# A windowed attention kernel: first q in two transfers, the other loads held behind it, the spare v copied last, and GpSimd drained behind its last store

## The chip, the cores and the metric

The kernel runs on one core of one Trainium2 chip. The metric is the device time of one execution in microseconds (us). Times are quoted as medians with the number of runs. The kernel before took 962.15 us (median of 3 runs, 961.51 to 962.47).

Engine names are those of the profile: PE (matrix multiply), DVE (VectorE), ACT (ScalarE), POOL (GpSimd), SP (SyncE). "Landing" means the moment when the last of the 16 semaphore increments of a transfer arrives; the trace records each increment with its time. A "hole" is idle time of the 16 DMA engines, given as their mean idle share summed over time; the "tail" is the time from the last landing to the end of the span, and the "span" is the length of the profiled run.

## The reference, cut to what matters

```python
B, S, D, W = 4, 4096, 1536, 64          # q, k, v: (B, S, D) float32
q_w, k_w, v_w = (x.reshape(B, S // W, W, D) for x in (q, k, v))
logits = einsum('bnwd,bnud->bnwu', q_w, k_w) * D ** -0.5
attn = softmax(logits)                  # over each window of 64
out = einsum('bnwu,bnud->bnwd', attn, v_w)   # float32
```

Every window of 64 rows attends only to itself. There are 16384 rows; each row of q, k and v is read once and each row of the output written once, so the work per byte is small.

## The kernel before

The rows are cut into N = 32 units of 512 rows. For each unit PE transposes q and k (12 groups `g`, 6 of q and then 6 of k), forms the logits, ACT takes the exponential, PE multiplies by v, and DVE and ACT scale the result into one of three output buffers. DVE copies the even groups out of PSUM (the buffers `tp` into which PE writes), ACT the odd ones. GpSimd issues the loads, which cast from float32 to float16 on the way, and the stores. Loads of q, k and v for the next unit go into the buffers as they become free.

Three units (1, 2 and 31) get their v through another buffer, "spare v", because at that moment `v16` is still in use. DVE copies it into `v16`. Where this copy stands in DVE's order is one subject of the change:

```python
def vector_unit(u):
    ve = nc.vector
    for g in range(0, 2 * DC, 2):                 # DC = 6: g = 0, 2, ..., 10
        copy_out(ve, ve.tensor_copy, u, g)
        if g == DC - 2:                           # after the last q group of DVE
            src = {1: staged(1, 0), 2: vs, N - 1: vs}.get(u)
            if src is not None:
                ve.wait_ge(*((d_v1, 16) if u == 1 else (d_vs, 16 if u == 2 else 32)))
                ve.wait_ge(p_o[0], 6 * u)
                ve.wait_ge(p_o[1], 6 * u)
                ve.tensor_copy(out=v16[:, :, :], in_=src[:, :, :]).then_inc(g_v, 1)
    # ... reciprocals and scaling of the output (cut)
```

The start. The first q comes as raw float32 through SyncE into an output buffer and is cast by DVE and ACT; all other first loads are issued by GpSimd at once:

```python
with tc.tile_critical():
    nc.sync.dma_start(
        out=slots(outs[0], 0, SLOTS, SLOTS), in_=rows(qf, 0, SLOTS, SLOTS)
    ).then_inc(d_raw, 16)
    load("k", 0, k16, d_k)
    load("v", 0, v16, d_v)
    # ... ident (cut)
    load("q", 1, staged(2, 0), d_q1)
    load("k", 1, staged(2, 1), d_k1)
    load("v", 1, staged(1, 0), d_v1)
    load("v", 2, vs, d_vs)
    # ...
    for a, eng in enumerate((nc.vector, nc.scalar)):
        eng.wait_ge(d_raw, 16)
        copy = nc.scalar.copy if a else nc.vector.tensor_copy
        for i in range(a, SLOTS, 2):
            copy(out=q16[:, i, :], in_=outs[0][:, i, :]).then_inc(c_q[a], 1)
```

The end. The last unit's result goes out in five pieces (two by GpSimd, three by SyncE), SyncE waits for every store, the critical block closes (this drains the engines), and a second block clears the semaphores:

```python
    # still inside the first block; gp = nc.gpsimd, sy = nc.sync
    gp.dma_start(out=rows(of, base, R, R), in_=slots(o, 0, R, R)).then_inc(d_l[0], 16)
    # ... waits (cut)
    gp.dma_start(out=half[:, 0, :], in_=o[:, R, :]).then_inc(d_l[1], 16)
    # ... three stores of 256 KB by sy, waits of sy for all stores (cut)
with tc.tile_critical():
    # ...
    nc.gpsimd.sem_clear(range(lo, hi + 1))
```

The softmax here doesn't subtract the row's maximum and nothing guards it: scores larger than these inputs give would overflow.

## Time and profile before

| What | Value | Where it is read |
|---|---|---|
| time | 962.15 us | median of 3 runs |
| span of the profiled run | 960.4 us | head of the page |
| DMA busy | 9 tenths in 39 of 40 slices | slice strip |
| PE, ACT, DVE busy | 65%, 36%, 31% | busy table |
| HBM traffic | 302 MB read, 101 MB written, 419 GB/s | queue table |

First, the DMA strip of the page (busy tenths of each 1/40 of the span) and the line of the software queue in the queue table (packets, MB, share of the time of 16 engines), and the line of the chain that ended last, by engine:

```profile
DMA  9999999999999999999999999999999999999993
...
q0 software_dynamic: 26496, 249.31, 99.0%
...
DMA 3%; PE 3%; DVE 1%; ACT 1%; issue 0%; POOL 0%; ACTq 0%
```

The DMA strip shows 9 in every slice but the last. With the same bytes moved at the same rate, such a kernel can be shortened only where the DMA is not busy. So one looks at the edges. Here is the end, as stretches of time: start and end, length, busy time of PE, PEld, DVE, ACT and POOL with the number of instructions, granted clock of PE, DMA share, GB/s.

```profile
932.00:934.00 2.00, 2.00 (x20) 1.84 (x19) 0.69 (x1) 0.06 (x1) 0.00 (x0) 1.00 0.95 406
934.00:936.00 2.00, 2.00 (x20) 1.69 (x19) 0.00 (x0) 0.61 (x1) 0.00 (x0) 1.00 0.35 147
...
942.00:944.00 2.00, 1.45 (x8) 0.19 (x2) 1.22 (x3) 0.39 (x1) 0.00 (x0) 1.00 0.00 0
...
952.00:954.00 2.00, 0.00 (x0) 0.00 (x0) 0.00 (x0) 0.00 (x0) 0.00 (x0) 0.50 0.71 263
954.00:960.00 6.00, 0.00 (x0) 0.00 (x0) 0.00 (x0) 0.00 (x0) 0.00 (x0) 0.50 0.00 0
```

Two stretches stand out: from 934 to 945 the DMA has almost nothing to do while PE is still computing the last unit, and from 954 to the end no engine has any work. The reason for the first stands in the order of time of the last unit (start, length, engine, line, operation, operands, and in brackets the idle time before it and what ended it):

```profile
919.73 0.61 ACT L206 COPY xk<-tp 128x512 f32<-128x512 f32 x1 [1.26 <-PE tp L139]
...
925.54 1.76 DVE L232 COPY v<-vs 128x6144 f16<-128x6144 f16 x1 [7.42 <-DMA vs<-in_v_dram]
927.22 0.68 DVE L206 COPY xk<-tp 128x512 f32<-128x512 f32 x1
...
928.05 1.08 PE L139 MATMUL tp<-ident,k 128*128 128x128 f32 x4 [8.36 <-DVE xk L206]
...
944.58 0.57 POOL L372 DMA_DIRECT2D out_dram<-out  x1 [29.05 <-PE o L114]
```

DVE waits 7.42 us for v with k's copies behind it, and PE waits 8.36 us for the k copy, although nothing in k needs v.

The reason for the second stretch is a wait of SyncE, in the view of waits (engine and line, who was waited for, us in total, times, longest):

```profile
SPq L293 <- POOLq L293: 4.1, 1, 4.1
```

This is SyncE waiting for GpSimd's drain at the close of the block. The trace has the drain as a record of 4.31 us, from 954.25 to 958.56, directly behind the last landing (953.96).

The start, and GpSimd's issues of the third unit's q and of the fourth's (same columns):

```profile
0.96 0.38 SPq L295 DMA_DIRECT2D out<-in_q_dram  x1
...
1.48 0.67 POOL L107 DMA_DIRECT2D k<-in_k_dram  x1 [1.03 <-SPq L293]
...
16.59 1.28 ACT L322 ACT_TABLE_LOAD   x1 [16.59 <-DMA out<-in_q_dram]
...
20.80 5.83 PE L139 MATMUL tp<-ident,q 128*128 128x128 f32 x24 [20.80 <-SPq L334]
...
52.63 1.36 POOL L107 DMA_DIRECT2D q<-in_q_dram  x1 [46.93 <-PE tp L139]
...
76.46 1.78 POOL L107 DMA_DIRECT2D q<-in_q_dram  x1 [15.59 <-PE tp L139]
```

Raw q lands only at 16.5 us because it shares the engines with k's load, and the two q issues take 1.4 and 1.8 us instead of the usual 0.54. DVE copies the spare v at these moments (52.12 to 53.87 and 76.38 to 78.13 in the trace). The Trainium skill describes this ("SBUF — State Buffer", section "SBUF: two separate sides", the "DVE blocks DMA" trap): GpSimd cannot write descriptors while certain DVE copies hold the port that both share. The trace agrees: the two issues end 0.12 and 0.11 us after the copies do. Near 54 and 79 us the DMA has holes of together about 1.2 us (idle share summed over 0.05 us bins: 0.68 in 50 to 58, 0.48 in 74 to 82).

### The profile page before, as it was taken

How to read it: one execution, taken by the hardware profiler on the slowest of the kernel's cores; microseconds unless marked ns; L12 is line 12 of the kernel's file. 1: busy time of each engine (PE TensorE's matmuls, PEld its weight loads, DVE VectorE, ACT ScalarE, POOL GpSimd, SP SyncE). 2: the span in 40 equal slices, each digit the busy share in tenths (PEclk: the TensorE clock that was granted, in tenths of full speed). 3: DMA queues.
4: the chain of work that ended last, by engine and by line, in shares of the span. 5: the costliest groups of instructions: out<-in, count | busy, mean ns of one | idle time of the engine just before them, and what ended most of it. 6: DMA issues, size and time to landing. Idle time of an engine off the chain costs nothing. (4 is left out here: it accounts for less than half of the span.)

```text
span 960.4 us, 10207 instructions
## 1 busy us (share of the span) xinstructions
PE 627.1 (65%) x4096; PEld 348.2 (36%) x3328; DVE 300.8 (31%) x524; ACT 341.0 (36%) x643; POOL 82.8 (9%) x133
## 2 busy tenths in 40 slices
PE   1777767666667666676666676666776666866652
PEld 1444444323444233443233442334432334422340
DVE  1444323332233322233222333222333223332232
ACT  1444334333333333343333333333433333333312
POOL 1011111010111000110100110001100001100100
PEclk9999899898899898998888998989988989888978
DMA  9999999999999999999999999999999999999993
GB/s 256 215 203 254 278 283 278 281 250 249 281 282 277 275 236 268 280 281 280 259 242 279 281 279 277 246 257 281 281 280 272 241 268 282 282 276 256 243 327 139
DMA packets 27090, 253.40 MB, mean 264 GB/s; under 512 B 2112, under 2 KB 2112, under 8 KB 10816
## 3 DMA queue, kind: packets, MB, share of 16 engines
q0 software_dynamic: 26496, 249.31, 99.0%
q1 hardware_dynamic: 576, 3.93, 1.1%
q14 instruction: 16, 0.13, 0.0%
q8 instruction: 2, 0.03, 0.0%
HBM read 301.99 MB, written 100.66 MB: 419 GB/s over the span
## 5 line engine op out<-in xcount | busy, mean ns | idle before, releaser
L114 PE MATMUL o<-v,et 128*128 128x512 f16 x768 | 255.0, 451 | 208.9 <-PEq L178 153.8
L279 ACT ACTIVATE out<-o,rs 128x512 f32<-128x512 f32 x192 | 127.1, 686 | 273.3 <-DVE rs L240 195.2
L155 PE MATMUL lt<-xq,xk 128*128 128x256 f16 x1536 | 195.8, 275 | 0.0
L181 PEld LDWEIGHTS <-et 128*128 128x128 f16 x256 | 28.9, 113 | 414.7 <-issue 409.1
L155 PEld LDWEIGHTS lt<-xq,xk 128*128 128x128 f16 x1536 | 148.9, 97 | 23.4
L240 DVE RECIPROCAL rs<-sp 128x1 f32<-128x1 f32 x128 | 21.6, 169 | 430.3 <-PE sp L114 430.3
L139 PE MATMUL tp<-ident,q 128*128 128x128 f32 x768 | 104.7, 281 | 70.3 <-DVE xq L206 49.5
L249 DVE TENSOR_SCALAR out<-o,rs 128x512 f32<-128x512 f32 x192 | 138.4, 748 | 16.8 <-PE o L114 10.5
L139 PE MATMUL tp<-ident,k 128*128 128x128 f32 x768 | 113.1, 277 | 40.1 <-DVE xk L206 22.6
L139 PEld LDWEIGHTS tp<-ident,q 128*128 128x128 f32 x768 | 87.2, 144 | 103.5 <-issue 80.2
L206 ACT COPY xk<-tp 128x512 f32<-128x512 f32 x96 | 58.9, 614 | 166.4 <-PE tp L139 166.4
L265 ACT ACTIVATE et<-lt,zeros 32x128 f16<-32x128 f32 x256 | 91.7, 358 | 56.2 <-PE lt L155 53.0
L139 PEld LDWEIGHTS tp<-ident,k 128*128 128x128 f32 x768 | 87.1, 141 | 55.7 <-issue 53.9
L206 DVE COPY xk<-tp 128x512 f32<-128x512 f32 x96 | 66.4, 692 | 118.6 <-PE tp L139 118.6
L206 ACT COPY xq<-tp 128x512 f32<-128x512 f32 x96 | 59.1, 616 | 93.5 <-PE tp L139 93.5
L206 DVE COPY xq<-tp 128x512 f32<-128x512 f32 x96 | 66.1, 689 | 56.9 <-PE tp L139 56.9
L107 POOL DMA_DIRECT2D v<-in_v_dram x29 | 20.8, 716 | 461.4 <-PE o L114 461.4
L114 PE MATMUL sp<-ones,et 128*128 128x1 f16 x256 | 46.1, 180 | 0.0
L107 POOL DMA_DIRECT2D q<-in_q_dram x30 | 18.3, 610 | 170.3 <-PE tp L139 170.3
L107 POOL DMA_DIRECT2D k<-in_k_dram x31 | 16.9, 545 | 183.9 <-PE tp L139 182.9
L289 POOL DMA_DIRECT2D out_dram<-out x31 | 22.1, 713 | 17.9 <-DVE out L249 16.8
L322 ACT ACT_TABLE_LOAD x1 | 1.3, 1283 | 16.6 <-DMA out<-in_q_dram 16.6
(21 smaller groups left out, 19.5 us busy)
## 6 DMA issues: line engine op xcount, KB each, us to landing
out_dram<-out POOLq DMA_DIRECT2D x31, 3072.0 KB, 29.2
k<-in_k_dram POOLq DMA_DIRECT2D x31, 1536.0 KB, 22.3
q<-in_q_dram POOLq DMA_DIRECT2D x30, 1536.0 KB, 21.5
v<-in_v_dram POOLq DMA_DIRECT2D x29, 1536.0 KB, 18.9
out<-in_q_dram SPq DMA_DIRECT2D x1, 3072.0 KB, 15.6
vs<-in_v_dram POOLq DMA_DIRECT2D x2, 1536.0 KB, 39.6
out<-in_q_dram POOLq DMA_DIRECT2D x1, 1536.0 KB, 30.1
out<-in_k_dram POOLq DMA_DIRECT2D x1, 1536.0 KB, 36.8
```

The costliest lines, as they stand in the source:

```text
L107: nc.gpsimd.dma_start(out=slots(dst, 0, SLOTS, r), in_=rows(src, u * UR, SLOTS, r)).then_inc(s, 16)
L114: return nc.tensor.add_instruction(mybir.InstMatmult(name=nc.get_next_instruction_name(), engine=PE, ins=[low(rhs), low(w)], outs=[low(o)] ...
L139: ins = nc.tensor.transpose(tps[g % 2][:, r, j, :], pairs[:, c * P : (c + 1) * P], ident[:, :])
L155: ins = nc.tensor.matmul(lts[h][:, r, :, :], lhsT=halves(xk, c)[:, r, h, :, w], rhs=halves(xq, c)[:, :, h, :, w], start=(c == 0 and w == 0 ...
L181: ld = nc.tensor.ldweights(w)
L206: copy(out=dst, in_=tps[g % 2][:, :, :, :]).then_inc(f_c[g % 4], 1)
L240: ve.reciprocal(out=rs[:, n : n + 1], in_=sp[:, n : n + 1]).then_inc(n_r, 1)
L249: ve.tensor_scalar_mul(scaled(u, n, j), ops[j][:, :], scalar1=rs[:, n : n + 1]),
L265: ins = sc.activation(ets[h][s, :, :, s], lts[h][s, :, :, s], EXP, bias=zeros[s, :], scale=scale)
L279: sc.activation(scaled(u, n, j), ops[j][:, :], COPY, bias=0.0, scale=rs[:, n : n + 1]),
L289: gp.dma_start(out=rows(of, u * UR, SLOTS, R), in_=slots(outs[u % NO], 0, SLOTS, R)).then_inc(d_o[u % NO], 16)
L322: copy(out=q16[:, i, :], in_=outs[0][:, i, :]).then_inc(c_q[a], 1)
```

## The change

The intent: get q in first and start PE early; keep DVE's k copies from waiting behind v; let GpSimd's drain run while the last stores fly, and drop one barrier.

```diff
+    # start: q in halves, all other loads behind the first half, table load early
-        nc.sync.dma_start(
-            out=slots(outs[0], 0, SLOTS, SLOTS), in_=rows(qf, 0, SLOTS, SLOTS)
-        ).then_inc(d_raw, 16)
+        raw = rows(qf, 0, SLOTS, SLOTS).rearrange("p h (r d) -> p (h r) d", d=D)
+        for i, s in enumerate((d_r0, d_r1)):
+            sl = slice(2 * i, 2 * i + 2)
+            nc.sync.dma_start(out=outs[0][:, sl, :], in_=raw[:, sl, :]).then_inc(s, 16)
+        nc.gpsimd.wait_ge(d_r0, 16)
         load("k", 0, k16, d_k)
@@
+        nc.scalar.activation(rs[:, 0:1], zeros[:, :], EXP, bias=zeros[:, :], scale=1.0)
         for a, eng in enumerate((nc.vector, nc.scalar)):
-            eng.wait_ge(d_raw, 16)
             for i in range(a, SLOTS, 2):
+                eng.wait_ge(d_r1 if i > 1 else d_r0, 16)
@@ vector_unit: spare v behind all of DVE's copies
         for g in range(0, 2 * DC, 2):
             copy_out(ve, ve.tensor_copy, u, g)
-            if g == DC - 2:
-                src = {1: staged(1, 0), 2: vs, N - 1: vs}.get(u)
-                # ... waits and copy
+        src = {1: staged(1, 0), 2: vs, N - 1: vs}.get(u)
+        # ... the same waits and copy
@@ end: one block, drain behind GpSimd's last store
-    with tc.tile_critical():
+    with tc.tile_critical(no_gpsimd_drain=True):
@@
         gp.dma_start(out=half[:, 0, :], in_=o[:, R, :]).then_inc(d_l[1], 16)
+        gp.drain()
@@
             sy.wait_ge(d_l[i], 16)
-
-    with tc.tile_critical():
+        sy.sem_inc(done, 1)
+        gp.wait_ge(done, 1)
```

(The comment line at the top of the diff is an explanation, and semaphore names are cut.)

## The prediction

> **What bounds the kernel.** The DMA. The slice strip gives it 9 tenths in 39 of 40 slices, the queue table 99.0% for the software queue; PE is busy 65%. The bytes (302 MB read, 101 written) don't change, so only the edges can move.
>
> **The edges now**, from windows of 1 and 2 us: (a) no DMA until 2 us, then full; (b) holes of about 0.6 us at 54 and 0.4 us at 78 to 80; (c) most engines run dry at 934, share near 0 from 940 to 945; (d) last landing 954.0, then 6.4 us to the span's end (960.4).
>
> **Start.** Raw q shares the engines with the first k load and lands at 16.5 us; first transpose 20.8. Alone and split, its halves should land near 7 and 11 us, with the table load (1.28 us) out of the way: first transpose near 13. But k lands no earlier (same bytes ahead of it) and unit 1's q, k, v follow in the queue, so unit 0 ends only about 3 us sooner. That is enough to issue the next q before the queue empties, without a VectorE copy beside it (the issues at 52.6 and 76.5 took 1.36 and 1.78 us, usually 0.54), so holes (b) should go: −1.0. Against that, k is issued only near 7 us. Its first packet now comes 3.5 us after its issue ended (2.15), while q's second half keeps the engines busy until about 10: a new hole of 0 to 1.5 us, I say +0.8. The Trainium skill, "DMA: Bandwidth & Descriptors" (opening table), gives about 1 us to a GpSimd DMA's first byte; the last unit's first store here took 1.13, the cold first load more.
>
> **Last unit.** The chain of waits has 28.95 us on the last v load (landing 925.5). VectorE waits for it with k copies behind: PE idles from 919.7 to 928.0, its clock at 0.5. With the copy last, everything after moves up 7.9 us, plus about 1.3 because PE stays warm (its first groups took 1.08 and 1.71 us instead of 0.6 and 0.91). v (ready 927.3) no longer binds. The first final store issues near 935.3 instead of 944.6. But the DMA engines don't end together: the previous store's 16 landings run from 934.2 to 940.5, 11 within 0.7 us, five late. The final 3 MB need about 7.7 us on each engine, so the latest ends near 948, not 944.5. Worth −5.6, of a 9.2 us shift.
>
> **End.** GpSimd's drain (4.31 us) runs after the last landing. Issued behind its last store it should end under the stores' flight; merging the two critical blocks saves a barrier (about 0.5). The 6.4 us tail becomes about 2: −4.5, if the drain doesn't itself wait for the data to land.
>
> **Sum.** −1.0 + 0.8 − 5.6 − 4.5 = −10.3: 951.9 us, 8-in-10 range 948 to 957. That is 1.1%: within 2% 0.97, faster 0.02, slower 0.01.
>
> **What would show it.** First half of q landed by 7.5 us; first transpose at 12 to 14; DMA hole near 10 us below 1.5; none at 54 and 78; PE without the 8 us gap in the last unit; first final store at 935 to 937; last landing near 948.5; drain over before it; tail near 2 us.
>
> **What would make it wrong.** The drain waits for outstanding stores (+4); the late engine's lag differs or isn't what ends the run (±3); the cold start makes the hole at 10 us larger (+2); the later v copy in units 1 and 2 delays the third unit's loads (+1).

## The result, and the profile after

The kernel after took 949.92 us (median of 4 runs, 947.45 to 950.55) against 962.31 us of the kernel before (median of 4, 961.51 to 963.32). The ratio is 0.9866, with a 95% interval of 0.9846 to 0.9886: 1.3% less time, within the 2% that count as the same. A ratio here is always the mean time of one kernel's fast runs over that of the other's of the same rounds, so it is not quite the ratio of the medians. The profiled run has a span of 948.6 us.

The last unit after, in order of time:

```profile
918.02 0.61 ACT L206 COPY xk<-tp 128x512 f32<-128x512 f32 x1 [0.88 <-PE tp L139]
...
918.42 0.63 PE L139 MATMUL tp<-ident,k 128*128 128x128 f32 x4 [0.44 <-DVE xk L206]
...
923.54 1.76 DVE L231 COPY v<-vs 128x6144 f16<-128x6144 f16 x1 [1.08 <-DMA vs<-in_v_dram]
...
925.38 2.97 ACT L264 ACTIVATE et<-lt,zeros 32x128 f16<-32x128 f32 x8 [1.66 <-PE lt L155]
...
933.55 0.57 POOL L374 DMA_DIRECT2D out_dram<-out  x1 [19.38 <-PE o L114]
```

PE's gap has shrunk from 8.36 to 0.44 us, and DVE waits for v 1.08 us with no copy behind it. The first final store is issued at 933.55 instead of 944.58. Now the stretches at the end:

```profile
932.00:934.00 2.00, 1.35 (x7) 0.19 (x2) 0.95 (x3) 1.00 (x2) 0.45 (x1) 1.00 0.56 238
934.00:936.00 2.00, 1.43 (x8) 0.10 (x1) 0.92 (x3) 0.95 (x2) 0.12 (x1) 1.00 0.86 363
936.00:938.00 2.00, 0.00 (x0) 0.00 (x0) 0.65 (x1) 0.00 (x0) 0.54 (x1) 0.99 0.98 412
...
942.00:944.00 2.00, 0.00 (x0) 0.00 (x0) 0.00 (x0) 0.00 (x0) 0.00 (x0) 0.50 0.42 160
944.00:946.00 2.00, 0.00 (x0) 0.00 (x0) 0.00 (x0) 0.00 (x0) 0.00 (x0) 0.50 0.05 19
```

The line of SyncE's wait for GpSimd in the view of waits:

```profile
SPq L292 <- POOLq L292: 1.4, 1, 1.4
```

And the page's line of the chain that ended last, by engine:

```profile
PE 2%; DVE 1%; ACT 1%; issue 0%; ACTq 0%
```

The hole from 934 to 945 has become a dip around 933. The DMA term has left the chain of the last work. But look at 942 to 946: the share falls to 0.42 and then to 0.05 while the run is still waiting for stores. A share of 0.05 is less than one engine of 16. The landings confirm it: of GpSimd's last store, eleven of 16 increments arrive between 941.4 and 942.2 us, four between 942.2 and 943.2 and one at 945.2. The wait for the drain has shrunk from 4.1 to 1.4 us, not to nothing.

The start, and the issues of the third and fourth unit's q:

```profile
0.91 1.28 ACT L319 ACT_TABLE_LOAD   x1 [0.91 <-SPq L292]
0.96 0.86 SPq L297 DMA_DIRECT2D out<-in_q_dram  x2
...
7.48 0.80 POOL L107 DMA_DIRECT2D k<-in_k_dram  x1 [7.03 <-DMA out<-in_q_dram]
...
12.42 5.36 PE L139 MATMUL tp<-ident,q 128*128 128x128 f32 x24 [12.42 <-SPq L336]
...
52.00 0.54 POOL L107 DMA_DIRECT2D q<-in_q_dram  x1 [39.94 <-PE tp L139]
...
75.63 0.56 POOL L107 DMA_DIRECT2D q<-in_q_dram  x1 [15.31 <-PE tp L139]
```

The halves of q land at 7.2 and 10.8 us and PE starts 8.4 us earlier, but the issue of the third unit's q comes only 0.6 us earlier. The two issues take 0.54 and 0.56 us.

Where the 11.9 us of the span went can be read from three moments of the two traces:

| Moment | before | after | difference to here | added here |
|---|---|---|---|---|
| last landing of the store before the last unit's | 940.5 | 938.5 | −2.0 | −2.0 |
| last landing of all | 954.0 | 946.0 | −8.0 | −6.0 |
| end of the span | 960.4 | 948.6 | −11.9 | −3.9 |

### The profile page after: what moved, and what is told of

It reads as the page before. It is cut to its first block, busy times and chain, and to the rows that moved or that the text cites. A ratio compares the mean times of both kernels' runs of the same rounds, so it can differ in the third digit from the quotient of the medians.

```text
span 948.6 us, 10199 instructions
## 1 busy us (share of the span) xinstructions
PE 631.6 (67%) x4096; PEld 349.9 (37%) x3328; DVE 301.4 (32%) x524; ACT 341.2 (36%) x644; POOL 81.8 (9%) x133
## 5 line engine op out<-in xcount | busy, mean ns | idle before, releaser
L107 POOL DMA_DIRECT2D q<-in_q_dram x30 | 16.3, 542 | 163.1 <-PE tp L139 163.1
L288 POOL DMA_DIRECT2D out_dram<-out x31 | 22.1, 713 | 18.8 <-DVE out L248 17.8
L324 ACT CAST q<-out 128x1536 f16<-128x1536 f32 x2 | 2.9, 1472 | 6.9 <-DMA out<-in_q_dram 6.9
```

The costliest lines, as they stand in the source:

```text
L107: nc.gpsimd.dma_start(out=slots(dst, 0, SLOTS, r), in_=rows(src, u * UR, SLOTS, r)).then_inc(s, 16)
L288: gp.dma_start(out=rows(of, u * UR, SLOTS, R), in_=slots(outs[u % NO], 0, SLOTS, R)).then_inc(d_o[u % NO], 16)
```

## The experiments

There were three groups of four runs, each group on its own chip. "Fast" ratios are against the kernel before of the same rounds.

### One part of the change at a time

**The start alone.** The edit is the first part of the diff above, on the kernel before.

```diff
+        raw = rows(qf, 0, SLOTS, SLOTS).rearrange("p h (r d) -> p (h r) d", d=D)
+        # two transfers; nc.gpsimd.wait_ge(d_r0, 16) before the loads; early EXP on ScalarE
```

> The kernel before with only the start changed (q in two transfers, other loads held, table load early). Theory: the held loads cost 1.2 us (second v copy's load, the last of the first six, lands at 56.3 instead of 55.1), but unit 1 runs early enough that the hole at 54 us goes; net of about -0.5 to -1.5: 961 us. The last unit still has the idle PE of 8 us and the 6.4 us after the last landing. Rival: the holes go only because the v copy in units 1 and 2 is out of the way; then the hole at 54 stays here and the time is 963 to 963.5.

Measured: 961.59 us (4 runs), ratio 0.9993, interval 0.9976 to 1.0010: not distinguishable from nothing. The mechanism in the expectation was partly there, but the hole at 54 us shrank and did not go. The last of the first six loads landed at 56.4 us instead of 55.15, as expected; the holes were 0.35 and 0.26 us instead of 0.68 and 0.48, and in this profile the last v landed at 923.47 us instead of 925.52. But the first final store was issued only 0.64 us earlier (943.94 instead of 944.58). The reason is PE's clock. Stretches of the last unit in the kernel before, from which the clock is the third number from the end:

```profile
926.00:928.00 2.00, 0.00 (x0) 0.00 (x0) 1.91 (x2) 0.00 (x0) 0.00 (x0) 0.50 1.04 442
928.00:930.00 2.00, 1.95 (x9) 1.57 (x10) 0.69 (x1) 0.00 (x0) 0.00 (x0) 0.50 0.96 412
930.00:932.00 2.00, 2.00 (x15) 1.74 (x14) 0.00 (x0) 0.55 (x1) 0.00 (x0) 0.75 1.04 442
```

and with the start alone:

```profile
926.00:928.00 2.00, 2.00 (x10) 1.60 (x11) 0.69 (x1) 0.00 (x0) 0.00 (x0) 0.50 1.01 430
928.00:930.00 2.00, 2.00 (x11) 1.66 (x10) 0.00 (x0) 0.32 (x1) 0.00 (x0) 0.50 1.01 430
930.00:932.00 2.00, 2.00 (x12) 1.64 (x11) 0.00 (x0) 0.30 (x1) 0.00 (x0) 0.52 1.04 442
```

PE went back to work 2.05 us earlier (at 926.00 instead of 928.05), but the full clock came back at 931.91 instead of 930.98, so it spent 5.9 us at half clock instead of 2.9. The Trainium skill ("TensorE: Matmul & The Clock Gate", section "Part 1: The HAM clock gate") says that the window of about 3.4 us over which activity is judged is free-running; the traces agree, since the half-clock stretch in both is 10.24 us, three such windows, wherever PE's work began inside it. The kernel with only the end changed shows the same: v landed 1.31 us earlier than in the kernel before, the half-clock stretch was again 10.24 us, and the first final store was issued 0.67 us earlier. So while the idle gap in the last unit is there, an earlier v need not give an earlier end.

**The v copy alone.** The edit is the second part of the diff.

> The kernel before with only the v copy moved to the end of VectorE's copies. Theory: the last unit's first store issues 9 us earlier, but the late DMA engine allows only 6 us of it: last landing 6 us earlier, and the issues of q at 52.6 and 76.5 take 0.54 us, which shrinks the hole at 78: 955 to 956 us. Rival (the late engine does not matter, the stores follow the compute): 953. Rival (the early start is what fed the last unit): above 960.

Measured: 954.67 us (4 runs), ratio 0.9924, interval 0.9905 to 0.9944, which is 7.3 us of 962. The first final store was issued at 934.33 (10.25 us earlier), and the last landing came at 946.74 (7.2 us earlier, of which 1.25 us were there before the last unit's stores). The rival in which the stores simply follow the compute wanted 953 and is not met: 10.25 us in the issue became 7.2 us in the landing. The part of the theory about the hole at 78 us failed: GpSimd's two issues took 0.55 and 0.56 us, and the holes were still 0.37 and 0.45 us.

**The end alone.** The edit is the third part of the diff.

> The kernel before with only the end changed (drain behind GpSimd's last store, one critical block). Theory: the drain waits for the stores to land and ends about 1.4 us after the last landing, so 3.9 us come off: 958.4 us, with 2.5 us from last landing to end. Rival: a drain has a fixed cost of 4.3 us counted from the last landing, only the barrier goes: 961.5.

Measured: 957.74 us (4 runs), ratio 0.9953, interval 0.9937 to 0.9970. From the last landing to the end it is 2.69 us instead of 6.47. The theory holds; a drain that always costs 4.3 us after the last landing is refuted.

The product of the three single ratios, 0.9993 x 0.9924 x 0.9953, is 0.9870; the kernel after has 0.9866. The parts add.

### The end: what does the drain wait for?

**The drain behind everything.**

```diff
-        gp.drain()                 # behind GpSimd's last store
@@
         gp.wait_ge(done, 1)
+        gp.drain()
```

> The kernel after, with the drain moved behind the last wait of all. Theory: alone, after everything has landed, a drain takes 4.3 us; overlapped it ended 2.17 us after the landing of GpSimd's last store (three runs), so here 4.3 us follow the landing: end 5.5 us or so after the last landing instead of 2.6, 952.5 to 953 us. Rival (most of the end's gain came from merging the critical blocks): within 1 us of the kernel after.

Measured: 951.93 us (4 runs), ratio 0.9900, interval 0.9883 to 0.9916, and 5.62 us from the last landing to the end instead of 2.60. The theory holds, with a time just below its range. Of the 3.9 us that the tail lost, 0.85 are thus the merged blocks (6.47 to 5.62) and 3.0 the place of the drain.

**All stores of the last unit by SyncE, the drain behind GpSimd's store of the unit before.**

```diff
         u, base, o = N - 1, (N - 1) * UR, outs[(N - 1) % NO]
-        # two stores by gp, gp.drain(), three stores by sy
+        gp.drain()
+        # all five stores by sy, with the same waits
```

> The kernel after, with all stores of the last unit issued by SyncE and the drain right behind GpSimd's store of the unit before. Theory: the drain ends 2.17 us after the landing of that earlier store (938.5), near 941, well before the last landing, so only about 1.3 us of clearing and barrier follow the last landing instead of 2.6: -1.2 us, 948.5 to 949. Rival (the drain waits for every transfer in flight): 949.9, as the kernel after.

Measured: 947.56 us (4 runs, 947.24 to 948.57), ratio 0.9852, interval 0.9836 to 0.9869. From the last landing to the end it is 1.29 us. The gain is a little more than expected (948.5 to 949). The records of the drain in five traces show what it waits for:

```
kernel                  drain: start    took     end   landing of GpSimd's last store
before                        954.25    4.31  958.56   953.24
drain behind everything       944.48    4.31  948.79   943.57
end alone                     946.35    8.45  954.79   952.62
after                         935.98   11.38  947.36   945.19
last stores by SyncE          911.78   28.57  940.35   938.25
```

In the three rows where the drain was issued with a store of GpSimd in flight it ended 2.17, 2.17 and 2.10 us after that store's landing; in the two rows where everything had landed it took 4.31 us. In the last row the last unit's stores, which SyncE had issued, were still in flight until 944.32 when the drain ended at 940.35, so it waits for GpSimd's own transfers and not for all. How long after the landing it ends is not fixed, though: in the run with ACT issuing the stores (below) it ended 0.25 us after the landing of GpSimd's last store (974.50), and why is open. So, in the kernel after, putting the drain behind the last store does not hide it. It saves the difference between 4.3 us after everything and 2.2 us after GpSimd's last landing; putting it behind a store that lands earlier hid it fully here.

### The start: what do the held loads cost?

**The kernel after without the hold.**

```diff
-        nc.gpsimd.wait_ge(d_r0, 16)
```

> The kernel after, without GpSimd's wait on the first half of q. Theory: the 1.2 us late landings are the price of the wait (first software transfer met idle engines): without it the last of the first six loads lands at 55.2 again, but q's halves land near 10 and 16.5 and the first transpose starts near 18; unit 1 is later, so part of the hole at 54 comes back: within 1.5 us of the kernel after (949 to 951.5). Rival (holding the loads is what makes the start pay): 952 or more.

Measured: 951.06 us (4 runs, 950.77 to 954.08), ratio 0.9894, interval 0.9872 to 0.9916. The last of the first six loads landed at 55.72 us (after: 56.34), the first transpose began at 21.73 us (after: 12.42), and the hole at 54 us was back (0.63 us). The second half of q landed at 20.16 us and the loads at 55.72 us, where the theory had 16.5 and 55.2: dropping the hold took back only about half of the 1.2 us. The time is about 1 us above that of the kernel after and inside the range of the theory; the intervals of the two overlap, so the sign is not settled by this run.

**Held only until the first quarter.**

```diff
-        for i, s in enumerate((d_r0, d_r1)):
-            sl = slice(2 * i, 2 * i + 2)
+        for s, sl in ((d_r0, slice(0, 1)), (d_r1, slice(1, 2)), (d_r2, slice(2, 4))):
@@
-                eng.wait_ge(d_r1 if i > 1 else d_r0, 16)
+                eng.wait_ge((d_r0, d_r1, d_r2, d_r2)[i], 16)
```

> The kernel after, with q in three transfers and the other loads held only until the first quarter is in. Theory: k is issued near 5.4 us instead of 7.5 and its first packets meet busy engines: the last of the first six loads lands 0.8 to 1.2 us earlier than 56.3, time -0.5 to -1: 949 to 949.5. Rival (the 1.2 us are the price of small packets or of the split itself): no earlier landing.

Measured: 948.74 us (4 runs, 947.62 to 949.86), ratio 0.9862, interval 0.9845 to 0.9879. k was issued at 6.0 us instead of 7.5, and the last of the first six loads landed at 55.70 us, 0.64 us earlier than in the kernel after. PE started at 14.64 us, 2.2 us later than in the kernel after. Against the kernel after (0.9866 in its own rounds) there is no gain in time that can be told from noise.

**The kernel after without its start** (v copy last and the new end on the old start), and **the kernel after again** in the same rounds.

```diff
 # on the kernel before: the second and the third part of the diff, not the first
```

> The kernel before with the v copy last and the new end, but the old start: the kernel after without its start. Theory (the three parts add, the start is worth about 0.5 to 1 us): 962.3 - 7.5 - 4.4 = 950.4 us, 0.5 to 1 above the kernel after of the same rounds. Rival (start worth nothing): the same as the kernel after; rival 2 (start worth its 2 us of earlier landings): 952.

> The kernel after, unchanged, to be compared with the others of these rounds: 949.5 to 950.

Measured: 950.72 us (4 runs, 948.76 to 952.16), ratio 0.9881, interval 0.9866 to 0.9897, for the kernel without the start; 949.19 us (4 runs, 948.18 to 949.89), ratio 0.9863, interval 0.9848 to 0.9878, for the kernel after. The difference is 1.5 us in the medians, with overlapping intervals. The three comparisons of the start have the same sign (in medians: alone −0.5, without the hold +1.1, without the whole of it +1.5; by the ratios −0.7, +2.7 and +1.7), but none is clear of the noise. So the start's worth is not shown; if it has one, these runs put it at 0.5 to 2.7 us. The early table load, one part of it, was not tested alone.

The traces say more of the hole at 54 us than these times do. In the 13 profiles in which GpSimd issues the stores before the last unit's, its size goes with the moment at which GpSimd's issue of the third unit's q ended, whether that issue was slow or quick: 0.68 us of hole for 53.99 (before, issue of 1.36 us), 0.63 for 53.88 (after without the hold, 0.55 us), 0.37 for 53.42 (v copy alone, 0.55 us), 0.27 for 53.28 (end alone, 1.36 us), 0.09 for 52.57 (after without its start) and at most 0.03 for 52.54 or earlier (every kernel with both the hold and the late copy). So the copy beside the issue is one way to be late, not the cause by itself.

### The last unit alone

```diff
-            if g == DC - 2:
+            if g == DC - 2 and u < N - 1:      # units 1 and 2 as before
@@
+        if u == N - 1:
+            # ... the same waits and copy, behind all copies
```

> The kernel before with the v copy moved to the end in the last unit alone. Theory (the last unit is what the later copy pays for): within 1 us of 954.7, which the copy moved in all three units gave; holes at 54 and 78 us as before, with GpSimd's issues of q there of 1.4 and 1.8 us again. Rival (a sizeable part came from units 1 and 2): 956 or more.

Measured: 955.31 us (5 runs, 954.71 to 955.72), ratio 0.9924, interval 0.9911 to 0.9938: the same ratio as with the copy moved in all three units. GpSimd's issues in the second and third unit were slow again:

```profile
52.04 1.52 POOL L107 DMA_DIRECT2D q<-in_q_dram  x1 [46.34 <-PE tp L139]
...
76.02 1.78 POOL L107 DMA_DIRECT2D q<-in_q_dram  x1 [15.59 <-PE tp L139]
```

So the quicker issues in units 1 and 2 are real and are worth nothing that these runs can show; what the later copy earns, it earns in the last unit.

### The late DMA engine

The expectation of 953 us for stores that follow the compute failed, so what does the end follow? These are moments of the traces (us; "last v" and "last of all" are landings):

| kernel | first final store issued | last v | last of all | from last v to last of all |
|---|---|---|---|---|
| before | 944.58 | 925.52 | 953.96 | 28.4 |
| start alone | 943.94 | 923.47 | 953.32 | 29.9 |
| end alone | 943.91 | 924.21 | 953.30 | 29.1 |
| v copy alone | 934.33 | 924.30 | 946.74 | 22.4 |
| v copy in the last unit alone | 934.22 | 924.18 | 946.60 | 22.4 |
| after | 933.55 | 923.52 | 945.96 | 22.4 |
| held until a quarter | 931.63 | 921.88 | 944.29 | 22.4 |
| after without its start | 931.93 | 921.88 | 944.40 | 22.5 |

With the copy last, the end stands 22.1 to 22.5 us behind the last v in all ten such profiles with the stores before the last unit's on GpSimd's queue. From the issue of the first final store to the last landing it takes 9.4 us in the three kernels with the copy early, where the engines are empty by then, and 12.4 to 12.9 us in these ten: about 3 us of waiting for a late engine. Everything queued behind v runs back to back there: the last landings of v, of the stores of units 29 and 30 and of the last store of all are at 923.52, 931.11, 938.54 and 945.96 us in the kernel after, in steps of 7.6, 7.4 and 7.4 us for 3 MB each. (That it is the same engine each time is inferred from the steps; the trace does not name it.) In the same trace eleven engines had finished unit 30's store by about 935.4, and the first final store was issued at 933.55, 5 us before the late engine was free for it. By this reading more speed in the last unit's compute would now gain nothing until the spread of the engines is smaller; no run tests that.

**Do the engines fall behind because of the software queue?**

```diff
 def store(u):
-    gp = nc.gpsimd
+    gp = nc.scalar           # called behind scalar_unit(u), for u < N - 1
```

> The kernel after, with all stores but the last unit's issued by ScalarE on a hardware queue. Theory: the late DMA engines (16 landings of one transfer spread over 6 us at the end) fall behind because of work tied to GpSimd's software queue; with half of the traffic off it the spread at the end should be about half, 3 us, and the end 2 to 3 us earlier: 947 us. Rival (the engine itself is slow, whatever the queue): spread of 6 us again and 950 us; rival 2: mixing queues delays the loads, over 952.

Measured: 975.86 us (median of 4 runs, 967.58 to 993.7, one of them slow), ratio of the fast runs 1.0088, interval 1.0049 to 1.0127. The 16 landings of the last v now lay within 2.2 us (in the kernel after: 5.6 us), those of unit 30's store within 1.3 us (5.9 us), but the kernel was slower and much more scattered, as the second rival had it. The theory cannot be called shown: in this run the DMA had holes of about 7 us in all after the first 82 us (kernel after: 0.14), and in a hole an engine that is behind can catch up (in the kernel before, the spread was 1.16 us in the load that landed at 55 us and 0.71 us in the next transfer, behind the hole at 54). The Trainium skill ("DMA: Bandwidth & Descriptors", section "Latency and other measured facts") says that two of the 16 engines are usually slower, with the software queue's descriptor rings as its guess. In these traces more than two are late: of the store before the last unit's, five landings in the kernel before came 1.9 us or more behind the other eleven, and eight in the kernel after came 1.6 us or more behind the first eight. The traces do not name the engines. The cause stays open.

### The two small gains together

The quarter hold and the last stores by SyncE, together:

```diff
 # the two edits above, on the kernel after
```

> Held until the first quarter of q, and the last unit's stores issued by SyncE with the drain behind the unit before, together: -0.6 from the first and -1.8 from the second against the kernel after: 947 us. If the first of the two was noise: 947.6, as the second alone.

Measured: 947.90 us (4 runs, 947.76 to 949.96), ratio 0.9854, interval 0.9839 to 0.9869, beside 0.9863 (0.9848 to 0.9878) of the kernel after in the same rounds. It took 1.29 us from the last landing to the end instead of 2.60, as the last stores by SyncE alone did (947.56 us, 0.9852). So the 1.3 us at the end are shown by the trace; nothing is left for the quarter hold, and the second alternative of the expectation holds. The simplest version that beats the kernel before, and by its tail the kernel after, is the kernel after with the last unit's stores on SyncE and the drain one store earlier. In time its lead over the kernel after is about 1 to 2 us and the intervals overlap, so in time that lead is not shown.

## Why the prediction was right or wrong

The total was right: 951.9 us predicted, range 948 to 957, 949.92 measured. By its own terms:

- **The bound.** Right. The middle of the kernel did not change; all of the gain came from the edges.
- **The start, sight by sight.** Right: first half of q by 7.5 us (7.2), first transpose at 12 to 14 (12.42), no hole at 54 in the kernel after (0.00 us in 50 to 58). The cost was mis-sized and looked different: it was put at +0.8 us as a hole near 10 us. The hole was 0.1 us, but twelve of the first 16 packets of k took 1.4 to 2.4 us each instead of about 0.93, and the first loads landed 1.2 us later. The slow packets are not shown to be the reason: in the second profile of the kernel after, the first 16 took 0.93 to 1.64 us and the first loads landed later still (56.58); without the hold they took 0.93 to 1.08 us and half of the delay stayed. The reason is open.
- **Holes at 54 and 78: −1.0.** The step "so holes (b) should go" was half right: the issues got quick, the hole at 54 went, and 0.19 us stayed at 74 to 82. What it is worth was not confirmed: moving the copy in units 1 and 2 gained nothing in time. The same holes also differ from run to run: the kernel with only the end changed, which is the same program up to 930 us, had 0.27 and 0.39 us instead of 0.68 and 0.48; and the kernels with the copy alone and with copy and end, which are the same program up to the last unit, had 0.37 and 0.45 us against 0.09 and 0.03. Start and holes together were predicted at −0.2 us; the three comparisons say −0.5 to −2.7, none clear of the noise, and the traces −2.0 in this pair. The last figure is not an effect of the change alone: the last v landed 1.3 us apart in two profiles of the same program (925.52, 924.21), and 2.1 us apart in the two profiles of the kernel after (923.52, 921.38).
- **Last unit: −5.6.** Right in mechanism and nearly in size: −6.0 in the pair of traces. The issue moved by 11.0 us (9.2 predicted; 2.0 of it came from the earlier landing of v), and the late engine gave only part of it back, as predicted. Its service of the final stores was put at 7.7 us and measured 7.4.
- **End: −4.5.** The wrong step is "Issued behind its last store it should end under the stores' flight". It did not. The doubt, that the drain waits for the data to land, was the truth, but its size (+4) was wrong: the drain ends 2.17 us after GpSimd's last landing, so the tail is 2.6 us instead of 2 and the gain 3.9 instead of 4.5.

Summed over this pair of traces, the part up to the last unit gave 1.8 us more than predicted, the last unit 0.4 more and the end 0.6 less: 1.6 us in the span, and 2.0 us between the predicted time and the median. The first of these, the largest, lies within the 2.1 us by which the two profiles of the kernel after differ: it is chance as far as the runs can tell. It also explains most of two sights that missed, the first final store at 933.55 us (935 to 937 predicted) and the last landing at 945.96 (near 948.5). The third, the drain that should be over before the last landing, missed by mechanism: it ended 1.4 us after it.

## What to carry to other kernels

When the DMA is full from end to end, work out for the last unit what each engine waits for in order: a copy that waits for the last load must stand behind everything that does not need it. Size the gain not by how much earlier the compute ends, but by when the slowest DMA engine is free for the store: here 10.25 us in the issue were 7.2 us in the landing. And put a drain of GpSimd behind a transfer of its own that lands early, giving the last stores to another queue.

## What the Trainium skill lacked or had wrong

- "DMA: Bandwidth & Descriptors", "Latency and other measured facts": it speaks of two slower engines. Here five to eight of 16 land late. The spread of one transfer's landings grows over the run, from 1.2 us at 55 us over 3.1 at 99 us to 6.35 us at 940 us in the kernel before, and with the copy last it sets the end of the kernel. The page says nothing of the growth.
- No page that I found tells what a GpSimd drain at the end of a kernel costs: 4.31 us with nothing in flight; with a store of GpSimd in flight it ended 2.10 to 2.18 us after that store's landing in eight of nine traces and 0.25 us after it in the ninth, and it did not wait for another queue's transfers.
